# Two-block kernel, chunked scan: u written beside the values, y and state as products of 128 rows, gate steps issued in twos

## The chip, the core and the metric

One NeuronCore of a Trainium2 chip runs the whole program: two transformer-like blocks over a sequence of 512 tokens of width 1024, in one launch. The metric is the device time in microseconds (us). Three runs of the kernel before took 2072.57, 2073.43 and 2083.99 us; the median is 2073.43 us.

Engines: PE is TensorE (PEld its weight loads), DVE is VectorE, ACT is ScalarE, POOL is GpSimd, SP is the engine that issues the DMAs. Each engine runs its own instructions strictly in the order in which they were issued and waits for others by semaphores.

## The reference

The part that the change touches is the RWKV-7 recurrence of the first block, 32 heads of 64 values, over 512 steps:

```
S_t = S_{t-1} diag(w_t) - (S_{t-1} kk_t) (a_t*kk_t)^T + v_t k_t^T ;  y_t = S_t r_t
y = head_group_norm(y);  y = (y + bonus) * silu(g);  out = y @ w_out
```

with r, k, v, g, w, a from products of the normed input, g = xg @ w_in[3]. The rest is an output product, a short convolution block, and a second block with a depthwise convolution, stick-breaking attention and a feed-forward of width 2816.

## The kernel before, in words

The program has four phases: `pre_phase` (norm, v), `chunk_phase` (r, k, decays, per-head factors, written to DRAM), `scan_phase` (the recurrence and the gate g, to about 711 us), `post_phase` (all the rest, beginning with the first output product, which reads y and silu(g) back from DRAM).

`scan_phase` treats the recurrence in 8 chunks of 64 steps (c = 0 to 7) for 8 *pairs* (q = 0 to 7). A pair is two tiles p of 128 features, that is four heads. Within a pair the chunks are a chain. One chunk goes so (lines of the kernel before; the products all go through `mm` on L1206):

- `v_mm`: products of the masked Gram matrix g with the tile VU, 128 rows deep, 4 into the Z half of the PSUM tile wy and 4 into the Y half. VU holds the values in 64 of its 128 rows; the other 64 (`own`) are cleared to zero by GpSimd (`clear_own`).
- `z_state`: 8 products of 64 rows with the old state St; `wn`: ACT copies the negated Z half to Wn.
- `s_old`: old state by an identity, and KBT with VU, into the PSUM tile us (128 rows each).
- `u_mm`: the inverted 64x64 triangle X with Wn, into us; `u_out` (L1263): DVE scales it to the tile UU, all 128 partitions in one instruction.
- `s_add`, `y_add`: 4 products each of 64 rows with UU, added to the state in us and to the Y half of wy; `s_new` (L1275): DVE makes the new state St.

After four chunks `y_out` copies the Y half out (ACT) and frees wy, of which there is one. Beside the chain, for the *next* pairs: `gram` and `mask` (L1169, DVE), `kbt`, and `inverse`, a serial DVE chain of 31 steps with two instructions each (xtmp on L654, X on L662) between two transposes (dn on L636, Xd on L683) and XT (L699), then two groups of 32 small products on PE with an ACT step between and behind (`ft_mm`, `h_mm`: ps_f, ps_h on L705). `u_mm` of a pair's chunk 0 needs the end of that pair's inverse. Group norm and bonus of a finished pair follow (mean, var, scale, V, yo).

The *gate* is filler for PE: 16 tiles, each of 8 steps `dense(k)` of three 128x128 by 512 products (ps_g, L1466 to L1468), with one PSUM buffer: the next tile waits for ACT's silu of the tile before. DVE makes the low halves of its weights (wl, L1457). Gate tile i may not begin before a given chunk's `u`.

The order on every engine is made ahead of time by `list_schedule` (L1510) from a table of assumed costs and handed to the program with no reordering. Steps of the chain have priority -100 and are "due"; another step is put into a gap on an engine only if its assumed cost, less a grace (`GRACE`, L1504), fits ahead of the next due step.

Of the kernel before, what the change touches and what calls it, by code (L numbers as in the profile page):

```python
# [778 lines left out]
def first_loads(nc, L, E):  # L779

    S, kz, iv = E["shared"][0], E["kz"], E["iv"]

    def ld(tag, src, p, bufs):
        def go():
            S[tag, p] = kz.tile([P, 1024], F32, tag=tag, name=tag, bufs=bufs)
            nc.sync.dma_start(out=S[tag, p], in_=src[p])
        return go

    def clear(p):
        def go():  # L790
            E["shared"]["VU"].append(iv.tile([P, NC, 2, C], F32, tag=f"VU{p}", name=f"VU{p}"))
            clear_own(nc, E["shared"]["VU"][p], p)
        return go

    def ld_v(p):
        def go():
            v_rows(nc, E["vD"], E["shared"]["VU"][p], p)
        return go

    for p in range(2):  # L800
        L.op("POOL", 1.1, clear(p), -5, (200, "clear", p))
        L.op("SP", 0.4, ld_v(p), 30, (200, "ld_v", p), [(200, "clear", p), (12, "dense", 0)], dma=0.7)
# [281 lines left out]
def scan_phase(nc, tc, A, E):  # L1084
# [7 lines left out]
    with ExitStack() as s:  # L1092
# [11 lines left out]
        def clear():  # L1104
            for p in range(2):
                clear_own(nc, Vs[2 + p], p)
        op("POOL", 2.2, clear, -1.0, (0, "clear"))

        def build(q):
# [36 lines left out]
            for p in range(0 if loaded else 2):  # L1146
                op("SP", 0.2, ld("KB", kbD, p, 2), q - 1.4, K("ld_kb", p),
                   [] if q == 0 else [(0, "kbt", p, 1)] if q == 1 else [(q - 1, "ld_kb", p)], [], ["KB"], dma=2.5)
                op("SP", 0.2, ld("ZR", zrD, p, 4), q - 1.4, K("ld_zr", p), [K("ld_kb", p)] + ([(0, "zs", NC - 1, y) for y in range(2)] if q == 2 else []), [], ["ZR"], dma=2.5)
                op("SP", 0.4, ld_v(p), q - 1.3, K("ld_v", p), [(0, "clear"), K("ld_zr", p)], [], ["VU"], dma=0.7)  # L1150
# [88 lines left out]
            def s_old(c):  # L1239
                def go():  # L1240
                    S["us"] = pc.tile([P, 2, 8, C], F32, tag="us", name="us")
                    for p in range(2):
                        for hd, hp in enumerate(HEADS):
                            if c:
                                mm(S["us"][hp, p, 2, :], ident[:, hp], S["St", c - 1][:, p, :], True)
                    for p in range(2):
                        for hd, hp in enumerate(HEADS):
                            mm(S["us"][hp, p, 2, :], S["KBT", p][:, c, hp], S["VU", p][:, c, hd, :], c == 0)
                return go

            def u_mm(c):
                def go():
                    if c == NC - 1:
                        S["us"] = pc.tile([P, 2, 8, C], F32, tag="us", name="us")
                    for hd, p, u, v in each(c):
                        mm(S["us"][u, 0, hd, :], S["X"][u, p, hd, c // 2, :], S["Wn"][u, hd, :], c == NC - 1 and hd == 0)
                return go

            def u_out(c):
                def go():  # L1260
                    S["U"] = st([P, 2, C], "UU", 2)
                    rn = sums[:, q, 0, c, :].rearrange("p (hd o) -> p hd o", o=1).to_broadcast([P, 2, C])
# [3 lines left out]
            def s_add(c):  # L1266
                def go():
                    for hd, p, u, v in each(c):
                        mm(S["us"][HEADS[hd], p, 2, :], S["KBT", p][u, c, HEADS[hd]], S["U"][u, hd, :])
# [9 lines left out]
            def y_add(c):  # L1279
                def go():  # L1280
                    for hd, p, u, v in each(c):
                        mm(wy(v, hd, c, 1), G(p)[u, hd, c, 1 - own(p, c), :], S["U"][u, hd, :])
# [14 lines left out]
            for c in range(NC):  # L1297
# [4 lines left out]
                opens = ("us", "u", c) if last else ("us", "s_old", c)  # L1302
                late = c in (0, 1, 2, 4, 5)
                op("PE", 0.5, v_mm(c), e if c % 4 == 0 else e - 0.115, K("v_mm", c),
                   [K("mask", p, b, hd) for p in range(2) for hd in range(2)] + ([K("y_out", 0)] if c == 4 else []) +
                   ([K("u", c - 1)] + ([K("y_add", c - 2)] if c % 4 > 1 else []) if c % 4 else []),
                   gg + vv + (w if c % 4 else []), [] if c % 4 else ["wy"], mode="h")
                if c:


                    for y in range(2):
                        op("PE", 0.15, z_state(c, y), e, K("zs", c, y), [K("zs", c, 0)] if y else [K("v_mm", c), K("s_new", c - 1)],
                           zs + [("St", "s_new", c - 1)] + w, mode="q")
                op("ACT", 0.3, wn(c), e, K("wn", c), [K("zs", c, 1) if c else K("v_mm", 0)], w, ["Wn"])
                if not last:
                    op("PE", 0.5 if c else 0.27, s_old(c), e + 0.005, K("s_old", c),
                       [K("zs", c, 1)] if c else [K("KBT", p, b) for p in range(2) for b in range(2)],
                       kk + vv + ([("St", "s_new", c - 1)] if c else []), ["us"], mode="h")
                op("PE", 0.26, u_mm(c), e, K("u", c),
                   [K("wn", c)] + ([] if last else [K("s_old", c)]) +  # L1320
                   ([] if c or not q else [K("h_out", 0), K("h_out", 1), K("place", 0)]),
                   ([] if q == 0 else ["X64"]) + [("Wn", "wn", c)] + ([] if last else [opens]), ["us"] if last else [],
                   mode="q")
                op("DVE", 0.3, u_out(c), e, K("u_out", c), [K("u", c)], [opens], ["UU"])
                op("PE", 0.25, y_add(c), e + 0.007, K("y_add", c), [K("u_out", c)] + ([K("u", c + 1)] if late else []),
                   gg + w + [("UU", "u_out", c)], mode="q")
                if not last:
                    op("PE", 0.15, s_add(c), e + 0.009, K("s_add", c),
                       [K("u_out", c)] + ([K("v_mm", c + 1)] if (c + 1) % 4 else []) + ([] if late else [K("y_add", c)]),
                       kk + [opens, ("UU", "u_out", c)], mode="q")  # L1330
                    op("DVE", 0.3, s_new(c), e, K("s_new", c), [K("s_add", c)], [opens], ["St"])
                if end:
                    op("ACT", 0.6, y_out(b), e + 0.04, K("y_out", b), [K("y_add", i) for i in range(4 * b, c + 1)],
# [102 lines left out]
        def gate():  # L1436
            def tile_ops(i):
# [23 lines left out]
                def dense(k):  # L1461
                    def go():
                        if k == 0:
                            S["ps"] = pd.tile([P, T], F32, tag="d", name="ps_g")
                        wh, wl = (S[n].rearrange("p (k f) -> p k f", k=KD) for n in ("wh", "wl"))
                        nc.tensor.matmul(S["ps"], wh[:, k, :], xg[0][:, k, :], start=k == 0, stop=False)  # L1466
                        nc.tensor.matmul(S["ps"], wh[:, k, :], xg[1][:, k, :], start=False, stop=False)
                        nc.tensor.matmul(S["ps"], wl[:, k, :], xg[0][:, k, :], start=False, stop=k == KD - 1)  # L1468
# [11 lines left out]
                when = [(int(at), "u_out", int((at % 1) * 8))] if i else []  # L1480
# [9 lines left out]
                op("ACT", 0.5, silu, p0 + 0.5, K("silu"), [K("dense", 7)], ["d"], ["sgt"])  # L1490
# [8 lines left out]
        emit_ops(nc, tc, L, dict(KB=2, ZR=4, V=1, VU=4, m=3, G=4, KBT=4, wy=1, UU=2, **INVERSE,  # L1499
# [4 lines left out]
GRACE = dict(PE=0.45, DVE=0.2, ACT=0.2, POOL=99.0, SP=99.0)  # L1504
# [608 lines left out]
```

## Time and profile before

| | us |
|---|---|
| median of three runs | 2073.43 |
| profiled execution, its own time | 2071.24 |
| span from first to last instruction | 2069.5 |
| PE busy | 1967.4 (95%) |
| DVE busy | 1046.2 (51%) |
| ACT busy | 838.8 (41%) |
| first product with VU / last `y_add` | 385.6 / 711.3 |
| first product of `post_phase` | 738.9 |

Busy is the union of an engine's records. Matmul records overlap each other: eight records (four products of float32 show as eight) of 0.22 us each can stand within 0.45 us. Times of instructions below are in us from the start of the span.

### The profile page before, as it was taken

The page shows a single profiled execution, that of the slowest core. Times are in us where ns is not written, and L with a number is a line of the kernel's source. Part 1 is how long each engine was busy: PE and PEld are TensorE (multiplying, and loading weights), DVE is VectorE, ACT ScalarE, POOL GpSimd, SP SyncE. Part 2 cuts the span into 40 slices and gives each one's busy share as a digit, 9 for nine tenths or more (in the row PEclk, how much of TensorE's full clock was granted, in tenths as well). Part 3 has the DMA queues.
Part 4 walks back from the last instruction along what each step waited for, and adds up shares of the span by engine and source line. Part 5 has one row for each costly group of instructions (what it writes and reads, how often), then busy time and mean ns, then how long its engine had stood idle before and what let it go on. Part 6 is the DMA issues. An engine that isn't in the chain of part 4 may idle for free.

```text
span 2069.5 us, 37138 instructions
## 1 busy us (share of the span) xinstructions
PE 1967.4 (95%) x15076; PEld 1579.5 (76%) x15076; DVE 1046.2 (51%) x2007; ACT 838.8 (41%) x1637; POOL 760.7 (37%) x660
## 2 busy tenths in 40 slices
PE   6989999799999979999999999996999999999998
PEld 5768888587778758888888887884667778888886
DVE  7958987688785342432332313797552442111101
ACT  5444554376655632322222223323765343223221
POOL 4220000001001135555555556753233565544442
PEclk9999999899999989999999999998999999999999
DMA  4445555634443383333333333331111523333321
GB/s 150 121 167 184 190 191 174 184 115 147 142 131 105 107 285 113 89 96 93 98 95 93 100 114 102 112 93 45 33 50 51 167 73 102 92 94 100 102 93 70
DMA packets 285763, 241.14 MB, mean 117 GB/s; under 512 B 14520, under 2 KB 236056, under 8 KB 285592
## 3 DMA queue, kind: packets, MB, share of 16 engines
q1 hardware_dynamic: 285592, 238.77, 37.2%
q8 instruction: 118, 1.93, 0.4%
q14 instruction: 53, 0.43, 0.1%
HBM read 198.89 MB, written 39.85 MB: 115 GB/s over the span
## 4 chain that ended last, share of the span: by engine, by line
PE 77%; DVE 13%; DMA 3%; issue 3%; ACT 2%; POOL 2%; SPq 0%; DVEq 0%; POOLq 0%; ACTq 0%
PE b L86 11%; PE b L85 11%; PE b L87 11%; PE b L120 6%; PE b L121 6%; DVE conv L1887 6%; PE b L119 5%; PE ps_d L940 3%; PE ps_d L941 3%; PE ps_d L942 3%; PE wy L1206 2%; PE us L1206 2%; PE ps_g L1466 1%; DVE X L662 1%; DVE xtmp L654 1%
## 5 line engine op out<-in xcount | busy, mean ns | idle before, releaser
L73 POOL TENSOR_TENSOR wl<-wr,wh 128x512 fp32r<-128x512 f32 (+1 forms) x463 | 641.4, 1408 | 615.1 <-ACT wh L65 613.8
L65 ACT CAST wh<-wr 128x1024 fp32r<-128x1024 f32 (+1 forms) x241 | 245.5, 1020 | 706.7 <-PE b L86 475.2
L87 PE MATMUL b<-s,wl 128*128 128x512 f32 x1024 | 404.1, 395 | 0.0
L86 PE MATMUL b<-s,wh 128*128 128x512 f32 x1024 | 404.0, 395 | 0.0
L85 PE MATMUL b<-s,wh 128*128 128x512 f32 x1024 | 403.1, 394 | 0.0
L85 PEld LDWEIGHTS b<-s,wh 128*128 128x128 f32 x1024 | 192.6, 188 | 47.0 <-issue 1.5
L86 PEld LDWEIGHTS b<-s,wh 128*128 128x128 f32 x1024 | 192.7, 188 | 45.7 <-issue 1.4
L87 PEld LDWEIGHTS b<-s,wl 128*128 128x128 f32 x1024 | 192.9, 188 | 43.6 <-issue 0.8
L119 PE MATMUL b<-wh,s 128*128 128x512 f32 x288 | 115.1, 400 | 13.9 <-ACT s L176 13.9
L1887 DVE SCALAR_TENSOR_TENSOR conv<-up,pkC,conv 128x512 f32<-128x512 f32 x120 | 117.1, 1042 | 0.4
L1359 POOL TENSOR_SCALAR var<-var 128x8 f32<-128x8 f32 x16 | 4.7, 293 | 305.9 <-ACT scr L1352 305.9
L120 PE MATMUL b<-wl,s 128*128 128x512 f32 x288 | 114.7, 398 | 0.0
L121 PE MATMUL b<-wh,s 128*128 128x512 f32 x288 | 111.1, 397 | 0.0
L2006 DVE TENSOR_TENSOR a<-sg,b 128x512 f32<-128x512 f32 x22 | 15.1, 688 | 172.5 <-PE b L87 164.3
L119 PEld LDWEIGHTS b<-wh,s 128*128 128x128 f32 x288 | 54.8, 190 | 27.8 <-ACT s L176 15.0
L1827 DVE TENSOR_TENSOR cu<-b,us 128x512 f32<-128x512 f32 x16 | 11.1, 692 | 124.3 <-PE b L87 119.0
L869 POOL MEMSET sg<- 128x8 f32 x16 | 1.7, 112 | 180.8 <-ACT pcl L893 162.7
L662 DVE TENSOR_TENSOR X<-X,xtmp 128x120 f32<-128x120 f32 (+24 forms) x248 | 65.0, 262 | 6.0
L654 DVE TENSOR_TENSOR xtmp<-dn,X 128x120 f32<-128x120 f32 (+24 forms) x248 | 64.8, 261 | 5.9
L121 PEld LDWEIGHTS b<-wh,s 128*128 128x128 f32 x288 | 54.8, 190 | 13.1
L120 PEld LDWEIGHTS b<-wl,s 128*128 128x128 f32 x288 | 54.8, 190 | 12.9
L1466 PE MATMUL ps_g<-xg_hi,wh 128*128 128x512 f32 x128 | 58.7, 459 | 2.0 <-ACT sgt L1473 2.0
(346 smaller groups left out, 4132.5 us busy)
## 6 DMA issues: line engine op xcount, KB each, us to landing
wr<-in_a_w_in SPq DMA_DIRECT2D x64, 512.0 KB, 4.6
wr<-in_b_w_in SPq DMA_DIRECT2D x64, 512.0 KB, 4.1
wr<-in_w_ffn_up SPq DMA_DIRECT2D x44, 512.0 KB, 3.9
wr<-in_w_in SPq DMA_DIRECT2D x36, 512.0 KB, 3.7
wr<-in_w_ffn_down SPq DMA_DIRECT2D x22, 512.0 KB, 3.5
kbD<-KB SPq DMA_DIRECT2D x16, 512.0 KB, 2.8
zrD<-ZR SPq DMA_DIRECT2D x16, 512.0 KB, 3.4
KB<-kbD SPq DMA_DIRECT2D x16, 512.0 KB, 4.5
```

The costliest lines, as they stand in the source:

```text
L65: copy = self.nc.scalar.copy(out=hi[:, :n], in_=raw[:, :n])
L73: eng.tensor_tensor(out=lo[:, sl], in0=raw[:, sl], in1=hi[:, sl].bitcast(F32), op=ALU.subtract)
L85: nc.tensor.matmul(ps, wh[:, k, :], xh[k], start=k == 0, stop=False)
L86: nc.tensor.matmul(ps, wh[:, k, :], xl[k], start=False, stop=False)
L87: nc.tensor.matmul(ps, wl[:, k, :], xh[k], start=False, stop=k == nk - 1)
L119: nc.tensor.matmul(pss[t], th, wh[:, k, :], start=s, stop=False)
L120: nc.tensor.matmul(pss[t], th, wl[:, k, :], start=False, stop=False)
L121: nc.tensor.matmul(pss[t], tl, wh[:, k, :], start=False, stop=e)
L654: nc.vector.tensor_tensor(out=tmp(i), in0=S["dn"][:, :, i:i + 1, 0:i].to_broadcast([P, 2, w, i]), in1=S["X32"][:, :, c:, i:i + 1].to_broad ...
L662: nc.vector.tensor_tensor(out=X, in0=X, in1=tmp(i), op=ALU.subtract)
L1206: nc.tensor.matmul(out, lhs, rhs, start=start, stop=True, skip_group_check=True)
L1887: nc.vector.scalar_tensor_tensor(out=conv[:, i, :], in0=up[:, i, tap:tap + T], scalar=col("conv_dw_w_2", tap * 4 + i), in1=conv[:, i, :], ...
```

## The change

- VU is no longer cleared. `u_out` writes u into the 64 rows of VU that were zero, in two DVE instructions of 64 partitions, one for each tile p. UU is gone.
- `v_mm` makes the Z half alone, 4 products of 64 rows. `y_mm` and `s_mm` take the place of the Y half of `v_mm`, of `y_add`, of the KBT half of `s_old` and of `s_add`: 4 products of 128 rows each, values and u at once.
- A small ACT copy `seen` is added before chunk 4 of each pair.
- Gate steps are issued two at a time (`RUN = 2`, six products), and PE's grace goes from 0.45 to 0.8.

```diff
-def clear_own(nc, t, p):
-    for h in range(2):
-        nc.gpsimd.memset(t[HEADS[own(p, h)], h::2, :, :].rearrange("p c hd f -> p c (hd f)"), 0.0)
...
                     for hd, p, u, v in each(c):
-                        mm(wy(u, hd, c, 0), G(p)[:, hd, c, own(p, c), :], S["VU", p][:, c, hd, :], c % 4 == 0)
-                    for hd, p, u, v in each(c):
-                        mm(wy(v, hd, c, 1), G(p)[:, hd, c, 1 - own(p, c), :], S["VU", p][:, c, hd, :])
+                        mm(wy(u, hd, c, 0), G(p)[v, hd, c, own(p, c), :], S["VU", p][v, c, hd, :], c % 4 == 0)
...
-                nc.vector.tensor_tensor(out=S["U"], in0=S["us"][:, 0, 0:2, :], in1=rn, op=ALU.mult)
+            def u_out(c, p):
+                def go():
+                    u = HEADS[own(p, c)]
+                    rn = sums[u, q, 0, c, :].rearrange("p (hd o) -> p hd o", o=1).to_broadcast([64, 2, C])
+                    nc.vector.tensor_tensor(out=S["VU", p][u, c, :, :], in0=S["us"][u, 0, 0:2, :], in1=rn, op=ALU.mult)
...
+            def s_mm(c):
+                def go():
                     for p in range(2):
                         for hd, hp in enumerate(HEADS):
-                            mm(S["us"][hp, p, 2, :], S["KBT", p][:, c, hp], S["VU", p][:, c, hd, :], c == 0)
+                            mm(S["us"][hp, p, 2, :], S["KBT", p][:, c, hp], S["VU", p][:, c, hd, :], c == 0 and p == 1)
...
+            def y_mm(c):
+                def go():
+                    for p in range(2):
+                        for hd in range(2):
+                            v = 1 - own(p, c)
+                            mm(wy(HEADS[v], hd, c, 1), G(p)[:, hd, c, v, :], S["VU", p][:, c, hd, :])
...
-                for k in range(KD):
-                    op("PE", 0.69, dense(k), p0 + k / 16, K("dense", k),
-                       [K("w_lo", k // 4)] + ([K("dense", k - 1)] if k else when),
+                for k in range(0, KD, RUN):
+                    op("PE", 0.69 * RUN, dense(k), p0 + k / 16, K("dense", k),
+                       [K("w_lo", k // 4)] + ([K("dense", k - RUN)] if k else when),
...
-GRACE = dict(PE=0.45, DVE=0.2, ACT=0.2, POOL=99.0, SP=99.0)
+RUN = 2
+GRACE = dict(PE=0.8, DVE=0.2, ACT=0.2, POOL=99.0, SP=99.0)
```

The order that the table makes of it differs at three places that matter here. In the rows, wy<-VU, us<-VU and wy<-UU are the products named above, us<-Wn is `u_mm`, wy<-St is `z_state`, us<-St the identity half of `s_old`; x4 is the number of equal rows.

PE, one chunk in the middle of the scan, before:

```order
L1206 MATMUL us<-UU,KBT 64x64 x4
L1466 MATMUL ps_g<-xg_hi,wh 128x512
L1467 MATMUL ps_g<-xg_lo,wh 128x512
L1468 MATMUL ps_g<-xg_hi,wl 128x512
L1206 MATMUL wy<-St,ZR 64x64 x8
L1206 MATMUL us<-St,ident 64x64 x4
L1206 MATMUL us<-VU_3911,KBT 64x64 x2
L1206 MATMUL us<-VU_3912,KBT 64x64 x2
L1206 MATMUL us<-Wn,X_5771 64x64 x4
L1206 MATMUL wy<-UU,g_3910 64x64 x4
```

and now (in place of the "..." the two rows ahead of it come once more):

```order
L1190 MATMUL us<-Wn,X_5824 64x64 x4
L1190 MATMUL wy<-VU_3907,g_3906 64x64
L1190 MATMUL wy<-VU_3908,g_3906 64x64
...
L1190 MATMUL us<-VU_3907,KBT 64x64 x2
L1190 MATMUL us<-VU_3908,KBT 64x64 x2
L1190 MATMUL wy<-VU_3907,g_3906 64x64 x2
L1190 MATMUL wy<-VU_3908,g_3906 64x64 x2
L1190 MATMUL wy<-St,ZR 64x64 x8
L1190 MATMUL us<-St,ident 64x64 x4
```

A full chunk has 28 products in place of 36, and the gate's three products that stood between the state's sum and `z_state` are gone from inside the chunk.

PE, around the last product of the scan's last chunk (pair 7, chunk 7), before:

```order
L1206 MATMUL us<-Wn,X_8419 64x64 x4
L1466 MATMUL ps_g<-xg_hi,wh 128x512
L1467 MATMUL ps_g<-xg_lo,wh 128x512
L1468 MATMUL ps_g<-xg_hi,wl 128x512
L1206 MATMUL wy<-UU,g_3910 64x64 x4
L1383 MATMUL tV<-ident,V 128x128 x4
```

and now:

```order
L1368 MATMUL tY<-ident,Y 128x128 x4
L1190 MATMUL us<-Wn,X_8428 64x64 x4
L1190 MATMUL wy<-VU_3907,g_3906 64x64 x2
L1190 MATMUL wy<-VU_3908,g_3906 64x64 x2
L1452 MATMUL ps_g<-xg_hi,wh 128x512
L1453 MATMUL ps_g<-xg_lo,wh 128x512
L1454 MATMUL ps_g<-xg_hi,wl 128x512
```

Of the gate's 384 products 336 stood ahead of the last y product and 48 behind it; now 126 stand ahead and 258 behind, the same triple again and again with one tV, tY between. Of the 126, 54 stand between the last chunk of pair 6 and the first u of pair 7.

DVE, at the end of the last inverse (XT of pair 7), before:

```order
L683 STREAM_TRANSPOSE Xd<-X_7880 128x8x8x4 x2
L1263 TENSOR_TENSOR UU<-us,sums 128x128
L699 STREAM_TRANSPOSE XT<-X_8419 128x512
L1169 TENSOR_TENSOR g_3909<-ps_g_8399,gmask 128x512
L1169 TENSOR_TENSOR g_3909<-ps_g_8400,gmask 128x512
```

and now:

```order
L1257 TENSOR_TENSOR St<-us,pcl 128x128
L683 STREAM_TRANSPOSE Xd<-X_7746 128x8x8x4
L1241 TENSOR_TENSOR VU_3162<-us,sums 64x128
L1241 TENSOR_TENSOR VU_3237<-us,sums 64x128
L699 STREAM_TRANSPOSE XT<-X_8428 128x512
L1388 TENSOR_TENSOR yo<-tV,yo 128x256 x2
```

The UU ahead of XT is chunk 7 of pair 5, the 48th of 64; the VU pair ahead of it now is chunk 7 of pair 6, the 56th. From the end of the chunk phase to this XT, DVE's list has 112 half u in place of 48 whole ones, 49 St for 42, 64 masks g for 50, 14 V for 10, 13 mu pairs for 11, 24 yo for 16, and 10 wl for 22; 434 steps of the inverse in both, of which 259 for 309 follow directly on the step on which they depend.

## Rows read from the trace of the kernel before

**Rows 1.** Windows: length, busy (records) of PE, PEld, DVE, ACT, POOL; clock; DMA.

```profile
389.50:630.70 241.20, 229.56 (x5003) 185.01 (x5003) 205.44 (x666) 147.31 (x428) 24.27 (x33) 1.00 0.45 130
630.70:711.30 80.60, 80.00 (x1553) 64.59 (x1552) 32.10 (x74) 47.58 (x146) 8.42 (x12) 1.00 0.34 100
```

**Rows 2.** DVE by line, 389.5 to 630.7: count | busy us, mean ns | idle before.

```profile
L662 DVE TENSOR_TENSOR X<-X,xtmp 128x120 f32<-128x120 f32 (+24 forms) x215 | 56.4, 262 | 5.4
L654 DVE TENSOR_TENSOR xtmp<-dn,X 128x120 f32<-128x120 f32 (+24 forms) x215 | 56.3, 262 | 5.3
L1169 DVE TENSOR_TENSOR g<-ps_g,gmask 128x512 f32<-128x512 f32 x43 | 27.9, 678 | 1.4 <-PE ps_g L1162 1.4
L1457 DVE TENSOR_TENSOR wl<-wr,wh 128x512 fp32r<-128x512 f32 x22 | 15.0, 681 | 0.9 <-ACT wh L1450 0.8
...
L1263 DVE TENSOR_TENSOR UU<-us,sums 128x128 f32<-128x128 f32 x48 | 13.6, 284 | 12.4 <-PE us L1206 12.4
L1275 DVE TENSOR_TENSOR St<-us,pcl 128x128 f32<-128x128 f32 x42 | 12.0, 285 | 3.9 <-PE us L1206 3.9
```

**Rows 3.** Timeline: the last XT.

```profile
629.97 0.71 DVE L699 STREAM_TRANSPOSE XT<-X 128x512 f32<-128x512 f32 x1 [0.50 <-ACT X L692]
```

**Rows 4.** Timeline: from the last y product to the first output product.

```profile
710.82 0.45 PE L1206 MATMUL wy<-UU,g 64*64 64x64 f32 x8
...
729.02 0.59 ACT L1473 ACTIVATE sgt<-ps_g 128x512 f32<-128x512 f32 x1
...
738.89 0.79 PE L119 MATMUL b<-wh,s 128*128 128x512 f32 x1 [11.27 <-ACT s L176]
```

**Rows 5.** Timeline of DVE: start, us; dependent steps, then independent ones.

```profile
495.07 0.29 DVE L654 TENSOR_TENSOR xtmp<-dn,X 128x126 f32<-128x126 f32 x1
495.39 0.29 DVE L662 TENSOR_TENSOR X<-X,xtmp 128x126 f32<-128x126 f32 x1
...
497.28 0.28 DVE L1263 TENSOR_TENSOR UU<-us,sums 128x128 f32<-128x128 f32 x1
497.48 0.81 DVE L1403 TENSOR_TENSOR yo<-tV,yo 128x256 f32<-128x256 f32 x2
```

**Rows 6.** Timeline of DVE: copies of 64 partitions, from 0 and then from 64.

```profile
363.63 0.16 DVE L1073 COPY sums<-rt 64x8 f32<-64x8 f32 x1
363.80 0.17 DVE L1072 COPY sums<-ps_s 64x8 f32<-64x8 f32 x1
```

**Rows 7.** Timeline of PE: the second group of an inverse.

```profile
456.88 1.80 PE L705 MATMUL ps_h<-X,FT 64*64 64x32 f32 x56
```

**Rows 8.** Timeline: one chunk of pair 7.

```profile
699.98 0.29 DVE L1263 TENSOR_TENSOR UU<-us,sums 128x128 f32<-128x128 f32 x1 [0.58 <-PE us L1206]
...
700.89 0.29 DVE L1275 TENSOR_TENSOR St<-us,pcl 128x128 f32<-128x128 f32 x1 [0.62 <-PE us L1206]
...
701.65 0.46 PE L1206 MATMUL wy<-St,ZR 64*64 64x64 f32 x16
...
702.32 0.40 PE L1206 MATMUL us<-VU,KBT 128*64 128x64 f32 x8
...
703.15 0.29 DVE L1263 TENSOR_TENSOR UU<-us,sums 128x128 f32<-128x128 f32 x1 [1.97 <-PE us L1206]
```

**Rows 9.** Timeline: gate steps, and the change from one gate tile to the next.

```profile
500.26 0.39 PE L1467 MATMUL ps_g<-xg_lo,wh 128*128 128x512 f32 x1
500.49 0.40 PE L1468 MATMUL ps_g<-xg_hi,wl 128*128 128x512 f32 x1
...
501.79 0.51 PE L1466 MATMUL ps_g<-xg_hi,wh 128*128 128x512 f32 x1 [0.90 <-ACT sgt L1473]
```

**Rows 10.** Windows: a stretch where the granted clock was 0.50 (columns as in rows 1).

```profile
375.00:385.00 10.00, 8.06 (x102) 6.54 (x103) 3.88 (x6) 1.82 (x3) 1.50 (x3) 0.50 0.11 44
```

**Rows 11.** Timeline: Gram products in that stretch, and later.

```profile
376.55 2.39 PE L1162 MATMUL ps_g<-ZR,KB 64*64 64x128 f32 x34 [11.43 <-DMA ZR<-zrD]
...
502.69 1.10 PE L1162 MATMUL ps_g<-ZR,KB 64*64 64x128 f32 x32
```

More of the change, by code (lines that the diff above doesn't have):

```diff
@@ L1102, in scan_phase @@
         Vs = E["shared"]["VU"] + [st([P, NC, 2, C], f"VU{b}") for b in (2, 3)]
[L1104 to L1107, printed above, removed]
         def build(q):
@@ L1242, in go @@
                     for p in range(2):
[L1243 to L1247, printed above, removed]
-                            mm(S["us"][hp, p, 2, :], S["KBT", p][:, c, hp], S["VU", p][:, c, hd, :], c == 0)
+                        for hp in HEADS:
+                            mm(S["us"][hp, p, 2, :], ident[:, hp], S["St", c - 1][:, p, :], True)
                 return go
@@ L1277, in s_new @@
                 return go
-            def y_add(c):
+            def y_mm(c):
                 def go():
-                    for hd, p, u, v in each(c):
-                        mm(wy(v, hd, c, 1), G(p)[u, hd, c, 1 - own(p, c), :], S["U"][u, hd, :])
+                    for p in range(2):
+                        for hd in range(2):
+                            v = 1 - own(p, c)
+                            mm(wy(HEADS[v], hd, c, 1), G(p)[:, hd, c, v, :], S["VU", p][:, c, hd, :])
                 return go
@@ L1301, in build @@
                 last, end = c == NC - 1, c % 4 == 3
-                opens = ("us", "u", c) if last else ("us", "s_old", c)
-                late = c in (0, 1, 2, 4, 5)
-                op("PE", 0.5, v_mm(c), e if c % 4 == 0 else e - 0.115, K("v_mm", c),
+                keep = 0 < c < NC - 1
+                opens = ("us", "s_old", c) if keep else ("us", "u", c)
+                op("PE", 0.23, v_mm(c), e - (0.115 if c % 4 else 0.0), K("v_mm", c),
                    [K("mask", p, b, hd) for p in range(2) for hd in range(2)] + ([K("y_out", 0)] if c == 4 else []) +
-                   ([K("u", c - 1)] + ([K("y_add", c - 2)] if c % 4 > 1 else []) if c % 4 else []),
-                   gg + vv + (w if c % 4 else []), [] if c % 4 else ["wy"], mode="h")
+                   ([K("u", c - 1)] if c % 4 else []),
+                   gg + vv + (w if c % 4 else []), [] if c % 4 else ["wy"], mode="q")
@@ L1308, in build @@
+                st_ = [("St", "s_new", c - 1)]
+                if c == 4:
+                    op("ACT", 0.2, seen, e, K("seen"), [K("v_mm", 4)], w)
+                if keep:
+                    op("PE", 0.25, s_old(c), e + 0.005, K("s_old", c), [K("zs", c, 1)], st_, ["us"], mode="h")
                 if c:
                     for y in range(2):
-                        op("PE", 0.15, z_state(c, y), e, K("zs", c, y), [K("zs", c, 0)] if y else [K("v_mm", c), K("s_new", c - 1)],
-                           zs + [("St", "s_new", c - 1)] + w, mode="q")
+                        op("PE", 0.15, z_state(c, y), e, K("zs", c, y), [K("zs", c, 0)] if y else
+                           [K("v_mm", c), K("s_new", c - 1)] + ([K("seen")] if c == 4 else []), zs + st_ + w, mode="q")
@@ L1314, in build @@
                 op("ACT", 0.3, wn(c), e, K("wn", c), [K("zs", c, 1) if c else K("v_mm", 0)], w, ["Wn"])
-                if not last:
[L1316 to L1331, printed above, removed]
+                op("PE", 0.26, u_mm(c), e, K("u", c),
+                   [K("wn", c)] + ([K("s_old", c)] if keep else []) +
+                   ([] if c or not q else [K("h_out", 0), K("h_out", 1), K("place", 0)]),
+                   ([] if q == 0 else ["X64"]) + [("Wn", "wn", c)] + ([opens] if keep else []), [] if keep else ["us"],
+                   mode="q")
@@ new lines, in build @@
+                done = [K("u_out", c, p) for p in range(2)]
+                for p in range(2):
+                    op("DVE", 0.23, u_out(c, p), e, K("u_out", c, p), [K("u", c)], [opens] + vv)
+                if not last:
+                    op("PE", 0.27, s_mm(c), e, K("s_mm", c), done + ([K("v_mm", c + 1)] if (c + 1) % 4 else [K("y_mm", c)]) +
+                       ([] if c else [K("KBT", p, b) for p in range(2) for b in range(2)]), kk + vv + [opens], mode="h")
+                    op("DVE", 0.3, s_new(c), e, K("s_new", c), [K("s_mm", c)], [opens], ["St"])
@@ L1332, in build @@
+                op("PE", 0.27, y_mm(c), e + 0.006, K("y_mm", c), done + ([] if end else [K("s_mm", c)]),
+                   gg + vv + w, mode="h")
                 if end:
-                    op("ACT", 0.6, y_out(b), e + 0.04, K("y_out", b), [K("y_add", i) for i in range(4 * b, c + 1)],
+                    op("ACT", 0.6, y_out(b), e + 0.04, K("y_out", b), [K("y_mm", i) for i in range(4 * b, c + 1)],
                        w + (["Y"] if b else []), [] if b else ["Y"])
```

41 lines of the change are left out of this document (17 added, 24 removed).

## The prediction

> **What bounds the kernel now.** I read the engine shares by window first. From 389.5 us to the end of the last inverse at 630.7, PE is busy for 229.6 of 241.2 us and DVE for 205.4 [rows 1]; from there to the last y product DVE works 32.1 of 80.6 us and PE all of it. By these figures PE is full throughout. The next view, DVE by line, shows why I don't take PE for the bound of the first stretch: of DVE's 35.8 idle us 10.7 are the short gaps between dependent steps of the inverse, so real waits come to about 25, of which 12.4 stand ahead of UU and 3.9 ahead of St [rows 2]. DVE does its list with 10% of waiting, and the list contains the serial inverse, 430 steps here. PE is full because gate products were put into every hole; a filled hole isn't a bound. The last XT ends at 630.7 [rows 3]; after it PE is the bound, since pairs 6 and 7 and the rest of the gate remain. The third view is the timeline at the end: last y product over at 711.3, last gate silu at 729.0, first output product at 738.9 [rows 4], with 11.27 us of PE idle ahead of it.
>
> The kernel is thus two stretches: DVE's list up to XT of pair 7, then what PE has left behind it. The change touches both, so I cost each.
>
> The Trainium skill ("Perfetto Trace Analysis", section "Identifying the Most-Contended Engine") says that matmul busy time is a bad measure of TensorE, and that the busy share of its weight loads should be used. The trace agrees: PEld has 185.0 of 241.2 us, less than DVE.
>
> **Stretch 1: DVE's list.** The end of XT(7) moves by what is added ahead of it in DVE's order (counts from the order, durations from the rows).
> - u: 48 whole ones become 112 halves, in turn from partition 0 and 64. The free size of a half is that of the whole, so its duration is still 0.284. A whole UU took 0.20 from its start to the next start (497.28 to 497.48), since it overlapped its neighbour [rows 5]; 48 of these are 9.6. Where two copies of 64 partitions change from the one half to the other they do not overlap: 363.63 plus 0.16 is 363.79, the next starts at 363.80 [rows 6]; they are small, so this is the nearest row and no proof. So I price a half at 0.305, a duration and the gap: 34.2, **+24.6**. If halves overlap as UU did, 22.4, +12.8.
> - 7 more St at 0.20, +1.4. 14 more masks g at 0.60 (0.678 less 0.08 of overlap), +8.4. 12 fewer wl at the same price, -7.2. 16 more small ones (8 yo, 4 V, 4 mu) at 0.40, half of the yo pair's 0.81, +6.4.
> - Fewer inverse steps follow directly on the step they need: 50 fewer. A dependent step costs 0.32 from start to start (495.07 to 495.39), an independent one about 0.11 less, -5.5.
>
> Work: +28. DVE's waits were 25. Gate triples leave the chunks and 480 records of products go, so waits of UU for PE should shrink; against that, the ps_f and ps_h groups, 1.8 us each [rows 7], and tV, tY now stand ahead of s_mm and u_mm. Neither is in the trace, so bounds are 0 and 45 (25 and ten late groups at 2); I take **18**, nearer to what the same list shows today. XT(7) then ends at 630.7 + 28 - 25 + 18 = 651.7, **+21**.
>
> The rule that speaks against the change is in the Trainium skill, "VectorE: DVE Perf Modes", section "Two Vector instructions with no wait between them": an instruction whose first input or output starts in another group of 32 partitions than the last access to that memory is held until all earlier Vector instructions have finished. By it the halves cost the +24.6; without it +12.8, and the forecast would be 2096. Rows 6 agrees with it, for copies of 8 elements.
>
> **Stretch 2: behind XT(7).** Before, it was 738.9 - 630.7 = 108.2. Now, in PE's order:
> - up to the first u of pair 7: 54 gate products at 0.23 (500.26 to 500.49) [rows 9], 12.4; two groups at 1.8, 3.6; some six hand-overs at 0.5 (St's end at 701.18 to z_state at 701.65 [rows 8]), 3. Together 19. This is a new stall: u_mm is queued behind the gate pieces, and DVE waits for it.
> - eight chunks of pair 7. A chunk took 3.17 (699.98 to 703.15) [rows 8]. The second u half adds 0.3; without a gate triple z_state can start about 0.25 earlier. The KBT products taken out at 702.32 lay beside ACT's Wn and are worth nothing. 7 periods and 1 us behind the last: 23.
> - 258 gate products at 0.23, 59.3. Between tiles PE waits for the silu, as there is one buffer: 500.49 to 501.79 is 1.30, so 1.07 more than a step [rows 9]. 9 tile changes are uncovered: 9.6. With tV, tY: 70. Group norm of pair 7 is hidden beside it.
> - from the last silu to the first output product 9.9, as before (729.02 to 738.89) [rows 4].
>
> Together 122, **+14**. The 48 gate products that followed the last y before lay partly beside the last pair's norm; 258 have nothing beside them that anyone needs, and the products taken out of the scan bring nothing while PE waits for DVE.
>
> **Sum.** +21 +14 = +35 on the profiled execution's 2071.24: 2106. The median of the runs is 2.2 above that execution, so on its basis **2108**. What follows the first output product is unchanged.
>
> **Rivals.**
> - *The other side: PE is the bound.* PE stands at 95% in rows 1. If PE's own time set the pace, each of 64 chunks would lose about 0.6 us (the KBT half of 0.40, and 8 of 16 records of a group like that of 0.46 at 701.65 [rows 8]; s_add and y_add become the new 128-row products), 38 us, and it wouldn't matter where the gate stands: 2035. It decides by the last y product: 70 + 10 stand behind it now, so before 659 the kernel is faster, before 638 by 1%. Against it: that XT(7) at 652 has 42 us of bridge and chain behind it; with no wait at all and overlapping halves it is at 622, and the last y product at 664. Chance 0.07.
> - *No change.* DVE's waits nearly vanish as PE empties, and halves overlap: work +16, waits 0 to 10, stretch 1 at -9 to +1; with +14, plus 5 to 15: 2078 to 2090. PE is then really idle, which speaks for it; the gate's bridge and tail remain. With non-overlapping halves and waits of 5, 2094. Chance 0.21.
> - *Slower still: the clock.* Where PE had been idle for 11.4 us the granted clock was 0.50, that is 1.2 of 2.4 GHz [rows 10], and a Gram group took 2.39 for 34 records where it took 1.10 for 32 later [rows 11]. In the changed scan PE has holes again. If the clock falls in pair 7's chunks alone, and half of each 3.17 is products (an estimate), 8 times 1.6: +13, 2121. If it falls through all 64 chunks, about 100. In the scan before it was 1.00 [rows 1]. Chance 0.05.
>
> The Trainium skill ("TensorE: Matmul & The Clock Gate") also ties the low clock to idle stretches of TensorE; rows 10 and 11 agree on the clock and on the doubled product time.
>
> **Chances.** The forecast with its bounds has 0.67. Low end: halves overlap, waits near 0, 2078; high end: waits 45 instead of 18, 2135, which also covers the clock in pair 7. Range **2078 to 2136**. Outside are the PE rival, a part of the no-change case and the clock through the scan, together under 0.2. One per cent, 21 us, is about what a measurement of this kernel can tell from no change: faster 0.07, same 0.21, slower 0.72 (forecast and clock).
>
> **What would show it.** XT of pair 7 ends near 652 and follows 56 chunks' u; two u halves start 0.30 apart, not 0.20; a chunk of pair 7 takes 3.2; the last y product ends near 694; then 258 gate products with gaps of about 0.9 <-ACT at each tile; first output product near 774. PE shows idle time in the scan where there was none. Wrong if the last y product ends before 659 (then PE was the bound), if DVE waits under 5 us up to XT(7), or if the clock in the scan falls below 1.00.

## The result, and the profile after

The changed kernel takes 2126.25 us (median of four runs, 2117.4 to 2129.1) against 2074.09: **slower, ratio 1.0231 with a 95% interval of 1.021 to 1.0252**. The forecast was 2108, range 2078 to 2136. The profiled execution took 2125.38 us, span 2123.7, 54.2 more than before.

Windows of the kernel after, columns as in [rows 1]: up to the end of the last XT, then to the first u of pair 7, to the last y product, and to the last gate silu.

```profile
389.50:661.30 271.80, 223.98 (x4789) 184.99 (x4790) 232.79 (x755) 162.82 (x499) 27.79 (x39) 0.91 0.38 115
661.30:680.20 18.90, 18.89 (x214) 15.18 (x214) 4.04 (x9) 12.20 (x34) 2.46 (x3) 1.00 0.20 61
680.20:705.70 25.50, 18.39 (x393) 14.50 (x393) 10.04 (x31) 10.06 (x37) 2.03 (x3) 0.88 0.21 61
705.70:780.30 74.60, 65.41 (x266) 49.94 (x266) 13.17 (x22) 25.86 (x50) 7.82 (x8) 0.97 0.40 127
```

DVE's share stayed about the same (85%, now 86%), PE's fell from 95% to 82%: PE now waits for DVE, which row 1 of [rows 1] hid behind gate products. By the view of waits for the first window (who waited for whom: us in total, times, longest), these two make up 37 of PE's 48 idle us:

```profile
PE us L1190 <- DVE VU L1241: 22.3, 32, 2.1
PE wy L1190 <- DVE St L1257: 14.9, 31, 1.6
```

The granted clock (the third figure from the end) was 1.00 in the whole scan before and is 0.91 in the first window here, which is 48 of its 272 us at 0.50. In the last window PE works on little but the gate, and the output waits for it.

DVE by line in the first window, columns as in [rows 2]:

```profile
L1153 DVE TENSOR_TENSOR g<-ps_g,gmask 128x512 f32<-128x512 f32 x57 | 38.8, 681 | 0.2
L1241 DVE TENSOR_TENSOR VU<-us,sums 64x128 f32<-64x128 f32 x110 | 31.5, 286 | 16.6 <-PE us L1190 14.7
...
L1257 DVE TENSOR_TENSOR St<-us,pcl 128x128 f32<-128x128 f32 x49 | 13.8, 282 | 5.6 <-PE us L1190 5.1
```

A half u lasts 0.286 us, as long as a whole one did (0.284). Its waits, with those of St, are still the largest.

DVE's timeline, two pairs of halves among steps of the inverse (start, us; x2 is both halves):

```profile
471.51 0.27 DVE L662 TENSOR_TENSOR X<-X,xtmp 128x100 f32<-128x100 f32 x1
471.69 0.58 DVE L1241 TENSOR_TENSOR VU<-us,sums 64x128 f32<-64x128 f32 x2
472.31 0.26 DVE L654 TENSOR_TENSOR xtmp<-dn,X 128x96 f32<-128x96 f32 x1
...
475.51 0.28 DVE L654 TENSOR_TENSOR xtmp<-dn,X 128x120 f32<-128x120 f32 x1
475.83 0.59 DVE L1241 TENSOR_TENSOR VU<-us,sums 64x128 f32<-64x128 f32 x2
476.34 0.27 DVE L662 TENSOR_TENSOR X<-X,xtmp 128x120 f32<-128x120 f32 x1
```

The first pair overlaps the step ahead of it by 0.09 (471.78 against 471.69) and leaves a gap of 0.04 behind; in the second pair it is the other way round. The first belongs to an even chunk, whose halves start at partition 0 and then 64; the second to an odd one, 64 and then 0. Over all 64 pairs the second half starts 0.302 (median) after the first; in even chunks 21 of 32 first halves overlap the instruction ahead and no second half the one behind, in odd chunks no first half and 29 second halves do.

Timeline of the end, PE and ACT: the first gate products behind the last y product, later ones with a change of tile, the last gate product and the last silu, the first output product. Compare [rows 4] and [rows 9].

```profile
704.68 1.00 PE L1190 MATMUL wy<-VU,g 128*64 128x64 f32 x8 [0.40 <-DVE VU L1241]
705.61 0.80 PE L1452 MATMUL ps_g<-xg_hi,wh 128*128 128x512 f32 x1
706.20 0.63 PE L1453 MATMUL ps_g<-xg_lo,wh 128*128 128x512 f32 x1
706.63 0.63 PE L1454 MATMUL ps_g<-xg_hi,wl 128*128 128x512 f32 x1
...
717.83 0.39 PE L1453 MATMUL ps_g<-xg_lo,wh 128*128 128x512 f32 x1
718.06 0.39 PE L1454 MATMUL ps_g<-xg_hi,wl 128*128 128x512 f32 x1
...
719.14 0.50 PE L1452 MATMUL ps_g<-xg_hi,wh 128*128 128x512 f32 x1 [0.69 <-ACT sgt L1459]
...
778.22 0.40 PE L1454 MATMUL ps_g<-xg_hi,wl 128*128 128x512 f32 x1
778.44 1.99 ACT L65 CAST wh<-wr 128x1024 fp32r<-128x1024 f32 x2 [5.72 <-DMA wr<-in_a_w_out]
780.34 0.59 ACT L1459 ACTIVATE sgt<-ps_g 128x512 f32<-128x512 f32 x1
...
789.67 0.79 PE L119 MATMUL b<-wh,s 128*128 128x512 f32 x1 [11.05 <-ACT s L176]
```

The last y product ends at 705.7, 5.6 us *earlier* than before. Then PE does 258 gate products, 0.23 apart (0.43 in the first four us), with a wait for the silu at each change of tile, and the first output product starts 84.0 us behind the last y instead of 27.6. These two, -5.6 and +56.4, are the whole change of the scan; 3.4 more lie behind the first output product (1334.0 against 1330.6; the kernels tried below have 1328.7 to 1332.6). Of these, 2.9 arise between 658 and 912 us behind that product, where the clock was 0.50 for 13.7 us in place of 6.8.

### The profile page after: what moved, and what is told of

The parts are those of the page before. It is cut to its first block, busy times and chain, and to the rows that moved or that the text cites. A ratio compares the mean times of both kernels' runs of the same rounds, so it can differ in the third digit from the quotient of the medians.

```text
span 2123.7 us, 35292 instructions
## 1 busy us (share of the span) xinstructions
PE 1974.1 (93%) x14116; PEld 1586.4 (75%) x14116; DVE 1060.4 (50%) x2071; ACT 839.7 (40%) x1645; POOL 753.1 (35%) x652
## 4 chain that ended last, share of the span: by engine, by line
PE 74%; DVE 14%; issue 4%; DMA 3%; ACT 2%; POOL 2%; SPq 1%; POOLq 0%; DVEq 0%; ACTq 0%
PE b L86 11%; PE b L85 11%; PE b L87 11%; PE b L120 5%; PE b L121 5%; PE b L119 5%; DVE conv L1874 4%; PE ps_d L929 3%; PE ps_d L930 3%; PE ps_d L931 3%; DVE X L662 2%; DVE xtmp L654 2%; DVE g L1153 1%; DVE VU L1241 1%; POOL wl L73 1%
## 5 line engine op out<-in xcount | busy, mean ns | idle before, releaser
L119 PE MATMUL b<-wh,s 128*128 128x512 f32 x288 | 115.3, 400 | 13.7 <-ACT s L176 13.7
L1190 PE MATMUL wy<-VU,g 128*64 128x64 f32 (+1 forms) x1024 | 66.1, 241 | 7.8 <-DVE VU L1241 4.7
```

Of the source, the lines that this page charges most:

```text
L119: nc.tensor.matmul(pss[t], th, wh[:, k, :], start=s, stop=False)
L1190: nc.tensor.matmul(out, lhs, rhs, start=start, stop=True, skip_group_check=True)
```

## The experiments

My theory after the result: **the loss is the gate's tail**, that is the order which steps of two and the grace make, and not the new products. The rival: the new products and DVE's 64 extra instructions cost it, wherever the gate stands. The kernels below differ in the two numbers or in a few lines; in the diffs "-" is the changed kernel unless another is named.

| run | gate ahead / behind last y | last XT ends | last y ends | last y to first output | median us | ratio to before (95%) |
|---|---|---|---|---|---|---|
| before | 336 / 48 | 630.7 | 711.3 | 27.6 | 2074 | |
| after | 126 / 258 | 661.3 | 705.7 | 84.0 | 2126.3 | 1.021 to 1.025 |
| e1 new products, single, 0.45 | 276 / 108 | 650.0 | 713.3 | 40.8 | 2085.5 | 1.003 to 1.007 |
| e2 new, single, 0.8 | 366 / 18 | 645.7 | 703.5 | 27.7 | 2060.8 | 0.991 to 0.995 |
| e3 new, twos, 1.4 | 384 / 0 | 653.2 | 731.1 | 23.7 | 2086.5 | 1.004 to 1.008 |
| e4 old, twos, 0.45 | 192 / 192 | 641.4 | 688.8 | 69.8 | 2085.9 | 1.005 to 1.009 |
| e5 after, filled twice | 126 / 258 | 669.4 | 714.9 | 84.4 | 2129.9 | 1.023 to 1.029 |
| e6 old, single, 0.8 | 351 / 33 | 640.9 | 713.7 | 25.7 | 2071.6 | 0.996 to 0.999 |
| e7 e2, half u on ACT | 366 / 18 | 642.0 | 709.2 | 27.1 | 2068.3 | 0.995 to 0.998 |
| e8 e7, 1.0 | 384 / 0 | 639.8 | 715.5 | 24.8 | 2072.9 | 0.996 to 0.999 |
| e9 new, twos, 0.45 | 150 / 234 | 650.7 | 693.1 | 76.1 | 2107.1 | 1.014 to 1.019 |
| e10 new, single, 0.6 | 312 / 72 | 652.6 | 699.2 | 34.1 | 2065.9 | 0.994 to 0.997 |
| e11 new, single, 1.0 | 369 / 15 | 651.4 | 709.5 | 26.5 | 2066.5 | 0.994 to 0.998 |
| e12 after, filled once | 126 / 258 | 659.2 | 709.9 | 83.3 | 2121.0 | 1.018 to 1.027 |

The times of the stretches are from one profiled execution each, so two or three us between kernels say little; in e4, e9 and e11 that execution is 4 to 7 us away from the median. The ratios are to runs of the kernel before made beside each (medians 2074.1 to 2077.2). "Single" and "twos" are `RUN` 1 and 2, the number is PE's grace.

**e1, new products alone.**

```diff
-RUN = 2
-GRACE = dict(PE=0.8, ...
+RUN = 1
+GRACE = dict(PE=0.45, ...
```

Expected: 

> The changed kernel with the gate issued in single steps again (three products) and PE's grace at 0.45: the new products alone. The order has 276 gate products ahead of the last y product and 108 behind it, for 126 and 258. My theory (the tail of gate products is the loss): 150 products at 0.23 and 6 tile changes at 1.07 leave the tail, 41 us; inside the scan PE has holes of 0.4 to 0.9 us per chunk that take a triple of 0.69 with about 0.1 to 0.3 us of delay, so 2085 to 2100 us. Rival (the new products and the halves of u are the loss, wherever the gate stands): 2115 to 2126.

Measured 2085.5, in the theory's range and not in the rival's. 41 of the 52 us are gone with the gate's steps put back: the tail fell by 43.2 and the last y product came 7.6 later. The other 11 us stay: with the new products these same settings leave 60 more gate products behind the last y than before, and the tail is 13.2 longer than there.

**e2, single steps, grace 0.8.**

```diff
-RUN = 2
+RUN = 1
```

Expected: 

> The changed kernel with single gate steps and the grace of 0.8 kept: 366 gate products ahead of the last y product, 18 behind. My theory: 240 products at 0.23 and 10 tile changes at 1.07 leave the tail, 66 us; given back in the scan are about 0.2 us for each of some 120 triples, 25 us at most: 2060 to 2085, so near the kernel before or faster. Rival (products and halves): 2105 to 2126.

Measured 2060.8, the fastest of all, 13 us under the kernel before. Its windows, to the last XT, to the last y and to the first output product:

```profile
389.50:645.70 256.20, 247.73 (x4665) 187.52 (x4665) 233.51 (x748) 165.17 (x478) 26.67 (x36) 1.00 0.47 143
645.70:703.50 57.80, 57.00 (x965) 41.55 (x964) 24.73 (x64) 35.84 (x110) 8.77 (x11) 1.00 0.25 84
703.50:731.20 27.70, 7.53 (x34) 5.28 (x34) 3.25 (x7) 12.52 (x34) 9.41 (x9) 0.69 0.49 165
```

240 gate products more than after, 55 us of PE, stand ahead of the last y product, and it ends 2.2 us *earlier*. DVE's busy time up to XT is the same (233.5 and 232.8); what fell are its waits, from 25.9 to 10.0 by the view of waits, and the clock is 1.00. The two largest waits, 14.7 and 5.1 us in the changed kernel, are now:

```profile
DVE VU L1241 <- PE us L1190: 5.6, 8, 1.1
DVE St L1257 <- PE us L1190: 1.9, 4, 0.9
```

The timeline of PE and DVE in pair 7 shows where the triples lie:

```profile
673.77 0.50 PE L1452 MATMUL ps_g<-xg_hi,wh 128*128 128x512 f32 x1
673.87 0.59 DVE L1241 TENSOR_TENSOR VU<-us,sums 64x128 f32<-64x128 f32 x2 [2.94 <-PE us L1190]
...
674.67 0.45 PE L1190 MATMUL us<-VU,KBT 128*64 128x64 f32 x8
...
675.17 0.29 DVE L1257 TENSOR_TENSOR St<-us,pcl 128x128 f32<-128x128 f32 x1 [0.71 <-PE us L1190]
675.33 0.51 PE L1452 MATMUL ps_g<-xg_hi,wh 128*128 128x512 f32 x1
...
676.23 0.46 PE L1190 MATMUL wy<-St,ZR 64*64 64x64 f32 x16
...
678.40 0.59 DVE L1241 TENSOR_TENSOR VU<-us,sums 64x128 f32<-64x128 f32 x2 [1.72 <-PE us L1190]
```

One triple runs while DVE makes the halves, one while it makes St, one (677.01 to 677.90) during ACT's Wn. A chunk of pair 7 is then 4.5 instead of 3.0 us: three triples are 2.1 us of PE, and 1.5 of that shows. One triple a chunk costs less: in e10 the first chunks of pair 7, with one each, took 3.0 to 3.3 us. Ahead of XT the triples seem to lie beside DVE's other work; no run separates this from the clock.

**e3, twos that may stand in a chunk.**

```diff
-GRACE = dict(PE=0.8, ...
+GRACE = dict(PE=1.4, ...
```

Expected: 

> The changed kernel, gate steps still in twos, with PE's grace at 1.4 in place of 0.8, so that a piece of six products may stand inside a chunk: all 384 ahead of the last y product. My theory: 258 products and 10 tile changes leave the tail, 70 us; a piece of 1.39 us in a hole of 0.6 to 0.9 delays the chain by 0.5 to 0.8, 64 times, 32 to 50 us, part of which DVE's list hides: 2070 to 2105. If being issued in twos is itself the loss: 2126 or slower.

Measured 2086.5, inside the theory's range. No gate product is left for the tail (23.7), but the last y product is 25 us later: pieces of six delay the chunks; in pair 7 it is 5.9 us from u to u where 11 gate products lie between, and 3.05 in two chunks of the four that have none.

**e4, old products with gate steps in twos** (a diff to the kernel before).

```diff
-                for k in range(KD):
-                    op("PE", 0.69, dense(k), p0 + k / 16, K("dense", k),
+                for k in range(0, KD, RUN):
+                    op("PE", 0.69 * RUN, dense(k), p0 + k / 16, K("dense", k),
...
+RUN = 2
```

Expected: 

> The kernel before with the gate's steps issued in twos alone (old products, u apart, PE's grace still 0.45): 192 gate products ahead of the last y product and 192 behind, for 336 and 48. My theory: 144 products at 0.23 and 6 tile changes at 1.07 are added behind the scan, 40 us, and at most 15 come back in the scan: 2097 to 2114. Rival (products and halves of u): within 1% of the kernel before, 2060 to 2090.

Measured 2085.9, a miss: it lies under the theory's range and inside the rival's. The tail grew by 42.2, as expected (40), but the last y product came 22.5 earlier, where at most 15 were allowed for. So a longer tail is not the loss by itself; what counts is how much of it comes back ahead of the last y. With e1 and e9 (below) this makes a square at a grace of 0.45, each against the kernel before: new products alone +11 us, twos alone +11, both +33. Neither alone makes the loss, and the theory's "not the new products" is too strong: together they cost 11 more than the two added up. From e1 to e9, 20.2 of a tail longer by 35.3 came back; in the changed kernel, with a grace of 0.8, the tail is longer by 56.3 than in e2 and the last y product 2.2 later, so nothing did.

**e5 and e12, the same order with PE's wait filled.** In the timeline of after ps_f and ps_h of pair 6's start take twice their usual time, and DVE waits 3.2 for St and 2.8 for VU right there. Is the granted clock what made the waits larger than forecast? Behind each `u_mm` of chunks 1 to 6 (`FILL` is set beside `RUN`):

```diff
+                    if 0 < c < NC - 1:
+                        for _ in range(FILL):
+                            for p in range(2):
+                                for hp in HEADS:
+                                    mm(S["us"][hp, p, 2, :], ident[:, hp], S["St", c - 1][:, p, :], True)
```

Expected of e5 (FILL = 2): 

> The changed kernel with PE's wait for the two u halves filled: behind each u_mm of chunks 1 to 6 the four identity products of s_old are issued twice more (they write the same numbers to the same place), 8 short products of about 0.04 to 0.08 us in a wait of 0.7 to 0.9. The order of everything else is unchanged. Theory (the clock costs what the forecast missed: ps_f and ps_h took 3.6 us in place of 1.8 at 614 to 623, and the first gate products behind the last y were 0.43 apart in place of 0.23): the granted clock rises in the scan, and up to 8 us of DVE's waits and 5 us in the tail come back: 2111 to 2121. Rival (the waits come from the order, not the clock): 2126 to 2140, with up to 0.2 us more per chunk.

Expected of e12 (FILL = 1): 

> As the run with PE's wait filled, with half the filling: the four identity products of s_old once more behind each u_mm of chunks 1 to 6, about 0.3 us in a wait of 0.7 to 0.9, so that the products of u's successors are not held back. Theory (low clock makes the waits of DVE that the forecast missed, 26 for 18): where the granted clock comes back to 1.00 the groups ps_f and ps_h take 2.0 in place of 3.6, DVE's waits up to XT of pair 7 fall to 16 to 21 and the time is 2115 to 2122. Rival (they come from the order): waits of 24 or more, 2123 to 2131.

Measured 2129.9 and 2121.0. PE's timeline of after:

```profile
614.38 3.63 PE L705 MATMUL ps_f<-XT,Nq 64*64 64x32 f32 x64 [0.23 <-DVE XT L699]
...
619.53 3.57 PE L705 MATMUL ps_h<-X,FT 64*64 64x32 f32 x64
```

and its window there, granted clock 0.50, that is 1.2 GHz:

```profile
614.30:626.00 11.70, 11.22 (x179) 10.54 (x180) 5.45 (x18) 5.19 (x13) 0.00 (x0) 0.50 0.37 129
```

The same stretch of e12, timeline and window:

```profile
619.05 2.01 PE L705 MATMUL ps_h<-X,FT 64*64 64x32 f32 x64
```

```profile
615.80:626.00 10.20, 9.58 (x229) 8.20 (x224) 7.61 (x25) 7.00 (x17) 0.00 (x0) 1.00 0.52 175
```

With the clock at 1.00 here DVE's waits of this segment (from one XT to the next) fall from 9.9 to 6.1, and the segment from 47.0 to 43.4 us. So the clock cost about 4 us in this place. The total of waits up to XT hardly moved, 24.3 for 25.9; in e5 it rose to 32.3, and its time lies in the rival's range: its filling made a chunk of pair 7 0.5 us longer (3.5 for 3.0). And in e12 the clock was 0.50 in pair 7 instead (690 to 700), where a chunk took 4.4 us; its first one, at 1.00, took 3.4. e12's time lies in the theory's range, its waits in the rival's, and its interval takes in that of after: it settles that the clock doubled those groups, not what the low clock costs in all.

A cleaner price stands in e9, whose pair 7 has two like chunks without gate products, one at either clock:

```profile
666.65:669.50 2.85, 2.06 (x56) 1.58 (x56) 0.87 (x3) 2.56 (x13) 0.00 (x0) 1.00 0.00 0
673.26:677.02 3.76, 3.12 (x49) 2.65 (x50) 0.87 (x4) 2.78 (x9) 0.00 (x0) 0.50 0.02 4
```

That is 0.91 us in each 3.76 at the low clock. At this rate the 48 us of low clock ahead of XT in the changed kernel would cost some 11 us, an estimate; no run takes it away alone.

**e6, old products, grace 0.8** (to the kernel before: `PE=0.45` becomes `PE=0.8`).

Expected: 

> The kernel before with PE's grace at 0.8 alone: 351 gate products ahead of the last y product, 33 behind, for 336 and 48. Theory (what counts is how many gate products stand behind, and DVE's list): 15 products and part of a tile change less, 3 to 5 us: 2068 to 2073. Rival (the grace alone makes the gain of the run with new products and grace 0.8): 2058 to 2064.

Measured 2071.6, as the theory has it. Against e2, which has the same grace and the same single steps, the new products are 10 to 11 us faster: with the gate out of the tail they are a gain, shown at this one grace.

**e7 and e8, the second half of u on ACT,** in e2, and with grace 1.0.

```diff
...
+                    if p == ON_ACT:
+                        for hd in range(2):
+                            nc.scalar.activation(out=S["VU", p][u, c, hd, :], in_=S["us"][u, 0, hd, :], func=AF.Copy,
+                                                 scale=sums[u, q, 0, c, hd:hd + 1])
+                        return
...
+ON_ACT = 1
```

Expected of e7: 

> The new products with single gate steps and grace 0.8, and the second half of each u made by ACT in two activations in place of one DVE instruction, so that the halves run beside each other. Order: 366 gate products ahead of the last y product, 18 behind; 50 first halves of u ahead of XT of pair 7. Theory (DVE's list bounds the first stretch): some 50 halves at 0.3 leave DVE's list, 15 us, and XT of pair 7 ends near 630 to 635: 2045 to 2056. Rival (PE, 97% busy in that run's scan, is the bound by now): 2058 to 2066, XT of pair 7 near 645.

Expected of e8: 

> As the run with the second half of u on ACT, with PE's grace at 1.0: all 384 gate products ahead of the last y product. Theory: 18 products at 0.23 and a tile change leave the tail, 5 us, and triples delay the chain a little more: 2040 to 2058. Rival (each triple in a chunk delays the chain by 0.3 or more, and pairs 6 and 7 then end later): 2058 to 2075.

Measured 2068.3 and 2072.9: misses of the theory; e8 lies in its rival's range, e7 above both. In e7 DVE's busy time up to XT is 217.9 for 233.5, the 15.6 that were to leave, but XT ends only 3.7 earlier: DVE's waits rose from 10.0 to 21.9. The edit did not do what it was made for. The halves were to run beside each other, but the trace shows them one behind the other in all 64 chunks, ACT's behind DVE's in 45 and DVE's behind ACT's in 19:

```profile
673.97 0.28 DVE L1246 TENSOR_TENSOR VU<-us,sums 64x128 f32<-64x128 f32 x1 [1.50 <-PE us L1190]
674.29 0.51 ACT L1243 ACTIVATE VU<-us,sums 64x64 f32<-64x64 f32 x2 [0.54 <-DVE VU L1246]
```

From the start of one half to the end of the other, a u takes 0.83 us there where it took 0.59 in e2, and 7.1 us of DVE's waits are for ACT's half. So e7 and e8 do not test what DVE's list is worth beside a full PE; that stays open, and so does what holds the second half back.

**e9, e10, e11, more points of the grace.** After e1 and e2 a simple law seemed to hold: 0.277 us for each gate product behind the last y.

The diff is e10's; e11 has `PE=1.0`, and e9 keeps `RUN = 2` and has `PE=0.45`.

```diff
-RUN = 2
-GRACE = dict(PE=0.8, ...
+RUN = 1
+GRACE = dict(PE=0.6, ...
```

Expected of e9: 

> The new products with gate steps in twos and PE's grace at 0.45: 150 gate products ahead of the last y product, 234 behind. Theory: with the new products the time follows the number N of gate products behind the last y alone, at 0.232 for a product and 1.07 for a tile of 24, so 0.277 each: from 2060.8 at N = 18 (0.277 times 90 gave 2085.7 at N = 108, measured 2085.5; times 240 2127 at N = 258, measured 2126). For N = 234: 2120.6, within 5. Rival (the grace of 0.45 against 0.8, or the place of the bridges in the scan, counts for as much): over 2127 or under 2112.

Expected of e10: 

> The new products with single gate steps and PE's grace at 0.6: 312 gate products ahead, 72 behind. Theory (0.277 us for each product behind the last y): 2075.8, within 5. Rival (triples within the chunks cost so much that fewer of them are better): under 2068; or the bridges between pairs count: over 2083.

Expected of e11: 

> The new products with single gate steps and PE's grace at 1.0: 369 ahead, 15 behind. Theory: 2060.0 by the count; since the tail is no longer the limit at 18 (the last gate product ended 6 us ahead of the last silu there, and the first output product waited for the norm of the last pair), it gains nothing: 2058 to 2066. Rival (a triple put into holes that are too small delays the chain): 2066 to 2080.

Measured 2107.1, 2065.9 and 2066.5. The law for the whole time falls: off by 13 and 10 us in e9 and e10, which lie in the range of a rival each. (e9's profiled execution, 2100.6, is the shortest of its four.) e11's 2066.5 lies at the border of its two cases and tells nothing apart. What the table shows instead is two parts. *The tail* follows the count: from after and e1, (84.0 - 40.8) / 150 = 0.288 a product and 9.7 besides, which gives 77.1 for e9 (76.1) and 30.4 for e10 (34.1); under some 50 products it stays at 24 to 28. In e2 it is the norm of the last pair that the output waits for there: the last silu starts at 714.1, the norm's last step (yo) at 723.1, the first output product at 731.2. *The last y product* does not follow the count: with the new products and the gate in single steps or in twos between chunks it ends anywhere from 693 to 713, at 693.1 with 150 products ahead and at 703.5 with 366. What sets it stays open.

## Why the prediction was right, and where its sizes were off

- **Direction and place: right.** DVE's list, not PE, set the first stretch: PE's busy share fell to 82% and XT of pair 7 came later. Gate products in PE's holes were no bound; taken out of the holes they became one. The rival that PE's time sets the pace (2035) is out, by its own condition: the last y product ended at 705.7, not before 659.
- **DVE's work: +28 forecast, +27.4 busy measured** (232.8 less 205.4). The price of a half was 0.305 and is 0.302, and with it the no-change case, which needed halves that overlap, lost one of its two conditions. The Trainium skill ("VectorE: DVE Perf Modes", section "Two Vector instructions with no wait between them") holds here: an overlap of 0.09 stands only on that side of a pair where the half and its neighbour start in the same group of partitions, which the two pairs in DVE's timeline show.
- **Waits: 18 forecast, 25.9 measured.** This is the mis-sized term, 8 us by the view of waits and 10 by DVE's whole idle time (39.0 for 28.8); with it XT of pair 7 ended at 661.3 instead of 651.7. I expected PE's emptier queue to shorten the waits, and it did not: they were as large as before (24.0 by the same view). At one place the clock's fall made about 4 of them (e12), and at e9's price for a chunk the low clock ahead of XT comes to as much as the whole miss. The grouping of the gate is not what makes them: e1 (single steps) has 19.9, e9 and e3 (twos) have 19.6 and 19.5. In the seven orders of these products without filling they go with the granted clock up to XT: 25.9 at 0.91, 19.5 to 19.9 (e1, e3, e9) at 0.94 to 0.97, 15.7 and 14.2 in e10 and e11 at 0.99, 10.0 in e2 at 1.00. Whether the clock makes the waits, or holes in PE make both, no run separates.
- **Behind XT: +14 forecast, +20.2 measured.** The bridge took 18.9 (19), the eight chunks 25.5 (23; from the u of the seventh to that of the last 5.0, at the low clock), the tail 74.6 (70), silu to output product 9.4 (9.9). In the tail ten changes of tile, for nine, cost 1.07 to 1.84 each for the 1.30 I took; the nine products at the low clock made 2.0 more, and the last silu started 1.7 behind the last gate product, since ACT was casting weights (778.44 to 780.43), a term that I had at nothing.
- **The clock rival** was given 0.05 as a cause by itself. The clock did fall, 0.91 up to XT with stretches at 0.50, and this was underrated. A chunk at the low clock cost 0.9 us more (e9), not the 1.6 that I took; with the 48 us ahead of XT that makes some 11 us there, an estimate, neither the 13 of pair 7 alone nor the 100 of all chunks. The four runs of the changed kernel point the same way: 2117.4 us at a granted clock of 0.969, the mean over the whole execution, and 2125.4 to 2129.1 at 0.963 to 0.965, where the profiled execution of the kernel before has 0.980. The condition that I named for being wrong, a clock under 1.00 in the scan, was met without the time leaving the range.
- **Behind the first output product** 0 forecast, 3.4 measured, 1.4 above the longest of the other kernels.
- **That the number lies in the range is in part luck:** +54 in the profiled execution for +35, with misses of 10 up to XT, 6.5 behind it and 3.4 at the end, all to the same side. The range's upper end stood for waits of 45; they were 25.9, and the rest of the miss came from terms that had no room of their own.
- **Slips on record.** The no-change case's own terms add to 2078 to 2088, and to 2095 with waits of 5. Over the whole scan 480 products go, which show as 960 records. V lasts 0.68, not 0.40 (1 us for four). None moves the forecast by more than that one us.
- **My split hid the plain account.** I divided the time at XT and booked +21 for stretch 1. Much of that is chain work that was done earlier: 56 chunks ahead of XT instead of 48. Divided at the last y product it is -5.6 and +56.4. The scan did get shorter, with 210 fewer gate products in it (48 us of PE at 0.23); what was slower is the work left behind it.

e2 is the version that beats both: new products, single steps, grace 0.8, 2060.8 us. Its last y product ends 7.8 us before that of the kernel before and the tail is as long as there (27.7 and 27.6).

## What to carry to other kernels

Filler work that stands in an engine's holes looks like a bound in its busy share; before it is made coarser, look at the hole: here a chunk of the chain took one triple of 0.69 nearly for nothing (e10), a piece of 1.39 made it longer (e3), and a planner that may not put it there leaves it for the end. Divide the time at the point behind which nothing else is left to overlap (here the last y product), and count what stands behind it. Change one scheduling number and the products of a chain apart: here steps of two cost 65 us at a grace of 0.8 (the changed kernel against e2) and hid the 13 that the new products with single steps gain.

## What the runs showed that I had not expected

The granted clock fell to 0.50, that is 1.2 GHz, in stretches of 3.4 to 13.7 us of the changed kernel's scan; in the 7 to 14 us ahead of five of the six, PE had been busy for 69 to 84%. In kernels with nearly the same order the places differ (614 to 628 in after; 688 to 708 in e12). ps_f and ps_h took 3.6 there for 2.0. The Trainium skill ("TensorE: Matmul & The Clock Gate", section "Part 1: The HAM clock gate") ties the low clock to idle stretches. The traces agree in the main: in e2, with PE 97% busy up to the last XT, the clock was 1.00 until the last y product, and the changed kernel, at 82%, has 48 us of low clock up to XT; but e6, also at 97%, has 3.4 us of it.
